# Forming the second gate inside the output projection instead of inside the second expert pass

## The chip, the core and the metric

The kernel runs on one core of one Trainium2 chip. The metric is the device time of one execution in microseconds; lower is better. The core's engines run side by side, each through its own instructions in order: PE (TensorE, the matmuls), DVE (VectorE), ACT (ScalarE), POOL (GpSimd) and SP (SyncE), which here only issues transfers. Sixteen DMA engines move data between main memory and the on-chip memory.

## What is computed

One layer of a decoder trunk on x of shape (1, 512, 2048). A conditioning vector c gives six rows of 2048 numbers (shift1, scale1, gate1, shift2, scale2, gate2), each a product of silu(c) with a 2048x2048 block of `w_ada`:

```python
mod = jax.nn.silu(c) @ w_ada[l] + b_ada[l]
shift1, scale1, gate1, shift2, scale2, gate2 = [m[:, None, :] for m in jnp.split(mod, N_MOD, axis=-1)]
h = x * (1.0 + scale1) + shift1
y = hybrid_mixer(h, ...)                        # ends with "@ w_out": the output projection
x = layer_norm(ALPHA * x + gate1 * y, ln1_g[l], ln1_b[l])
h = x * (1.0 + scale2) + shift2
y = peer(h, peer_w_q[l], peer_sub_keys[l], peer_u[l], peer_v[l])   # product-key experts
x = layer_norm(ALPHA * x + gate2 * y, ln2_g[l], ln2_b[l])
```

The second gate, gate2, is needed only for the last line.

## The kernel before

The program is one long stream, written in order and placed on the engines by a scheduler that keeps each engine's own sequence fixed. Its stages, with the times they take in the profile: input modulation, projection, state-space heads and attention (0 to about 586 us); the output projection (586 to about 800); the queries of the expert layer (to about 1000); the first expert pass with `uT` (to about 2137); the second expert pass with `vT` (to about 3187); the last LayerNorm.

All large matmuls use float32 data cut into two parts. `split` copies a raw tile to `hi` on ACT (L189) and forms `lo = raw - hi` on DVE (L190); `mm3` then runs three matmuls (L196 to L198). So each chunk of weights needs a transfer, one ACT pass, one DVE pass, and then PE work.

**`ada`** forms one row of the modulation on DVE. It walks a column piece of `w_ada` in sixteen slices of 128 rows: SP loads a slice (L220, tile `wa`), DVE multiplies it by one number per partition and adds it to the accumulator `acc` (L225 for the first slice, L227 for the others). For a gate, PE then sums `acc` over the partitions (L243, tile `pc`), DVE adds the bias (L244, tile `grow`) and the row goes to main memory. `ada` is a generator: each `pump` lets it do one step, so its work is laid between other work. `pace[0]` ties a step behind the latest `lo`.

**The output projection** (L738 to L784) runs over eight groups, one for each pair of token blocks and each of four column blocks `dc`. A group has eight steps; a step loads 512 KB of `w_out` (L745, tile `wo`, a ring of four buffers), splits it and runs 24 matmuls of 512 columns into `po`. At a group's end DVE runs `t`, `xres` and `stats` (L771 to L774). `norm1` (L699 and on) normalises finished token blocks between the steps. From the second group on each step adds `RATE_S` to a counter and pumps the generator `shifting` by its whole part. `shifting` is the second half of shift2: sixteen slices of 512 KB, through a ring of two buffers (`ra0`, `ra1`), the slots that the tag "rawa" names in this stage.

**The second expert pass** (L1133 on) runs sixteen rounds `sg`; a round has four column blocks `dc` of two parts. A part loads 1 MB of `vT` (L1144, tile `wvv`) into the three-buffer ring "raw8", splits it in two halves (L189, L190) and runs 36 matmuls into `pv`. Between them DVE adds finished blocks to `yacc` (L1195), and adds rows that POOL gathers one by one (L857) to `h2t` (L822). Before the change, in rounds 2 to 9, each first part also pumps `gate2`, an `ada` over column pieces of 512, whose loads hold four slices each (1 MB) and take a buffer of the same ring "raw8".

Of the kernel before, what the change touches and what calls it, by code (L numbers as in the profile page):

```python
# [21 lines left out]
D = 2048  # L22
# [9 lines left out]
SHARE = (4, 4, 8, 8)  # L32
RATE_X = 2
RATE_Z = 2.5
RATE_S = 0.6
EARLY_Q = 6
TAIL = ((0, 1, 2, 3), (0, 2), (0,))
G_SCALE = 32768.0
# [77 lines left out]
def body(ctx, tc, I, out, dbg=None):  # L116
# [7 lines left out]
    ps = Ring()  # L124
# [10 lines left out]
    st = Ring()  # L135
# [28 lines left out]
    g2s = tc.dram_tile([1, D], F32, name="g2s")  # L164
# [82 lines left out]
    def run(gen):  # L247
        for _ in gen:
            pass

    pace = [None]

    def pump(gen, n):
        for _ in range(n):
            if next(gen, gen) is gen:
                return


    with ExitStack() as sa:
        mx = sa.enter_context(tc.tile_pool(name="mx", bufs=1))  # L260
        rt = Tags(sa.enter_context(tc.tile_pool(name="rt", bufs=2)), bT=1, cT=1, xdt=1, btok=1, cbm=1, hst=1, sc=1, sq=2, ada=1)
# [70 lines left out]
        due = [0.0]  # L332
# [27 lines left out]
        pieces = WAVE  # L360
# [317 lines left out]
    with ExitStack() as sb:  # L678
# [10 lines left out]
        hf = xb.tile([P, D], F32, name="hf")  # L689
        shifting = ada(st, ps, rt, 3, 2, shift2, 0.0, ((1024, 1024),))  # L690

        def queries(hc):

            if hc % 2 == 0:
                early_q.append(ps.tile([P, 512], F32, name="pq", tag="acc"))
            at = hc % 2 * 2 * P
            colgemm2(I["w_q"][hc], early_q[-1][:, at:at + 2 * P], 0, 2 * P, False)
# [40 lines left out]
        for tbs, dc in [(t, d) for t in ((0, 1), (2, 3)) for d in range(4)]:  # L738
            dsl = slice(dc * 512, (dc + 1) * 512)
            t1 = {}  # L740
            for half in (1, 0):
                pa = {b: ps.tile([P, 512], F32, name=f"po{b}", tag="acc") for b in tbs}
                for q in range(4):
                    raw = st.tile([P, 2, 512], F32, name="wo", tag="raw")
                    nc.sync.dma_start(raw, I["w_out"][dc, half * 2 + q // 2][:, q % 2 * 2:q % 2 * 2 + 2, :])  # L745
                    hi, lo, ins = split(st, raw, [P, 2, 512], "w")
                    pace[0] = ins.ins
                    for b in tbs:
                        sl = slice(b * P, (b + 1) * P)
                        for k in range(2):  # L750
                            kk = (1 - half) * 8 + q * 2 + k
                            mm3(pa[b], hhi[:, kk, sl], hlo[:, kk, sl], hi[:, k, :], lo[:, k, :],
                                q == 0 and k == 0, q == 3 and k == 1)
                    if dc or tbs[0]:
                        due[0] += RATE_S
                        pump(shifting, int(due[0]))
                        due[0] -= int(due[0])
                if tbs[0] and dc == 3 and half == 0:
                    for hc in range(EARLY_Q):
                        queries(hc)  # L760
                if half == 1:
                    if tbs[0] == 0:
                        nc.scalar.dma_start(g1[:, dsl], g1s[0:1, dsl].to_broadcast([P, 512]))
                    for b in tbs:
                        nc.scalar.dma_start(xres[:, b, dsl], I["x"][b * P:(b + 1) * P, dsl])
                for b in tbs:
                    if half == 1:
                        t1[b] = rt.tile([P, 512], F32, name="t1", tag="t1")
                        A.activation(t1[b], pa[b], AF.Copy, scale=rms[:, 4 + b:5 + b])
                        continue  # L770
                    V.scalar_tensor_tensor(t1[b], pa[b], rms[:, b:b + 1], t1[b], ALU.mult, ALU.add)  # L771
                    V.tensor_tensor(t1[b], t1[b], g1[:, dsl], ALU.mult)
                    V.scalar_tensor_tensor(xres[:, b, dsl], xres[:, b, dsl], ALPHA, t1[b], ALU.mult, ALU.add)
                    V.bn_stats(stats[:, b, dc, :], xres[:, b, dsl])  # L774
                    if dc == 3 and b >= 2:
                        norm1(b)
            if tbs[0] and dc == 0:
                run(shifting)
                V.tensor_tensor(gc, cols[:, C_L1G:C_L1G + 16], scale2, ALU.mult)
                V.tensor_tensor(bc, cols[:, C_L1B:C_L1B + 16], scale2, ALU.mult)  # L780
                V.tensor_tensor(bc, bc, shift2, ALU.add)
                norm1(0)
            if tbs[0] and dc == 1:
                norm1(1)  # L784


    front.close()
# [73 lines left out]
    with ExitStack() as sc_:  # L861
# [30 lines left out]
        for hc in range(16):  # L892
            pa = ps.tile([P, 512], F32, name="pa", tag="acc")
            c0 = 2 * P if hc < EARLY_Q else 0
# [156 lines left out]
        for i in range(U1):  # L1051
            hl = dense_u(i)
# [8 lines left out]
    with ExitStack() as sv:  # L1061
# [67 lines left out]
        ws[1] = weights(1)  # L1129
        bring(3)  # L1130
        g2 = None
        gate2 = ada(st, ps, rt, 5, 1, g2s, pieces=tuple((c0, 512) for c0 in range(0, D, 512)), n=4, tag="raw8")
        for sg in range(16):  # L1133
            last = sg == 15
            for dc in range(4):
# [4 lines left out]
                for part in range(2):  # L1140
                    gi = sg * 2 + part
                    hl = []
                    both = st.tile([P, 4, 512], F32, name="wvv", tag="raw8")
                    nc.sync.dma_start(both, I["vT"][gi, dc])  # L1144
                    for n in range(2):
                        raw = both[:, 2 * n:2 * n + 2, :]
                        if final and part + n == 2:
                            hi = rt.tile([P, 2, 512], F32R, name="hi", tag="w")
                            lo = rt.tile([P, 2, 512], F32R, name="lo", tag="gt")
                            hl.append((hi, lo, split_into(hi, lo, raw)))  # L1150
                        else:
                            hl.append(split(st, raw, [P, 2, 512], "w"))
                    hls += hl
                    if final:
                        continue
                    for b in range(ND):
                        sl = slice(b * P, (b + 1) * P)
                        for i in range(4):
                            hi, lo = hl[i // 2][:2]
                            mm3(pa[b], ws[gi][:, 0, i, sl], ws[gi][:, 1, i, sl], hi[:, i % 2, :], lo[:, i % 2, :],  # L1160
                                part == 0 and i == 0, part == 1 and i == 3)
                    if sg < 15 and (dc, part) in ((1, 1), (3, 1)) and sg * 2 + 4 + dc // 2 < 32:
                        bring(sg * 2 + 4 + dc // 2)
                    if not last and (dc, part) in ((1, 0), (3, 0)):
                        nx = sg * 2 + 2 + dc // 2
                        ws[nx] = weights(nx)
                    if sg > 1 and part == 0:
                        pace[0] = hl[1][2].ins
                        pump(gate2, 1)
                    if sg < 14:  # L1170
                        for n in range(1 + (part + dc == 4 or (sg % 4, dc, part) == (0, 1, 0))):
                            fetch(hl[n][1].bitcast(F32)[:, 0, 0:1], hl[1][2].ins, 1)
# [105 lines left out]
```

## Time and profile before

| | |
|---|---|
| runs of the kernel | 3220.56 us median of 3 (3210.94 to 3221.17) |
| the profiled execution | 3211.76 us, of which span 3210.1 us |
| PE busy | 3072.1 us (96% of the span) |
| DVE busy | 2626.2 us (82%) |
| ACT busy | 1292.0 us (40%) |
| POOL busy | 801.4 us (25%) |
| loads of `wa` by SP | 96 of 512 KB, 48 of 1 MB |

The profile is of one execution: each row of its trace is an engine's instructions, transfers, or the time in which an engine stood still and what ended the wait. A busy PE is not a PE at its peak, since matmuls overlap and their ends are modelled; the number of matmuls in a stretch says more than the busy share. The profiled execution is near the fastest of the three runs, 8.80 us under their median.

### The profile page before, as it was taken

Reading aid. Unit: us, or ns where it says so; the run is one execution under the profiler, and the core shown is the slowest. Engines: PE = TensorE matmul, PEld = TensorE weight load, DVE = VectorE, ACT = ScalarE, POOL = GpSimd, SP = SyncE. Lnnn points to the kernel's source line nnn. Section 1 sums busy time; section 2 is a strip of 40 time slices with the busy share of each in tenths; the row PEclk is TensorE's granted clock in tenths of the full one; section 3 lists DMA queues with packets and bytes.
Section 4 is the critical chain, followed back from the end, with each engine's and each line's share of the span. In section 5 each row is a group of like instructions: output and inputs, shape, how many; then the busy total and the mean of one; then the engine's idle time right before and its main releaser. Section 6 shows DMA issues by size and latency. Waiting matters only on the chain.

```text
span 3210.1 us, 43195 instructions
## 1 busy us (share of the span) xinstructions
PE 3072.1 (96%) x16241; PEld 2622.1 (82%) x16241; DVE 2626.2 (82%) x4091; ACT 1292.0 (40%) x2149; POOL 801.4 (25%) x651
## 2 busy tenths in 40 slices
PE   7889899899799999999999998999999999999997
PEld 3677577678788999999999998988777778788885
DVE  6677877686597999999999896868888889888887
ACT  2333335445422333475467774333222232223332
POOL 0000001001240154333432232322434334533301
PEclk9989999999899999999999999999999999999998
DMA  9654654586653599989998889998999989898862
GB/s 341 222 172 149 212 178 137 173 285 196 215 189 112 212 345 351 339 317 364 334 345 327 329 330 350 395 339 314 333 342 330 340 325 365 327 350 314 308 230 79
DMA packets 249426, 899.92 MB, mean 280 GB/s; under 512 B 19600, under 2 KB 113744, under 8 KB 173280
## 3 DMA queue, kind: packets, MB, share of 16 engines
q1 hardware_dynamic: 106624, 460.46, 39.7%
q0 software_dynamic: 41776, 303.12, 25.1%
q10 hardware_dynamic: 100816, 133.57, 12.4%
q8 instruction: 127, 2.08, 0.3%
q14 instruction: 83, 0.68, 0.1%
HBM read 834.87 MB, written 62.19 MB: 279 GB/s over the span
## 4 chain that ended last, share of the span: by engine, by line
PE 75%; DVE 8%; DMA 8%; issue 5%; POOL 1%; ACT 1%; SPq 0%; DVEq 0%; ACTq 0%; POOLq 0%
PE pa L198 11%; PE pa L196 11%; PE pa L197 11%; PE pv L197 9%; PE pv L198 9%; PE pv L196 9%; DMA wa<-w_ada 3%; DMA wvv<-vT 3%; DVE lo L190 2%; PE po L197 1%; PE po L198 1%; PE pg L1011 1%; PE po L196 1%; DVE acc L227 1%; POOL row L857 1%
## 5 line engine op out<-in xcount | busy, mean ns | idle before, releaser
L196 PE MATMUL pa<-hhi,hi 128*128 128x352 f32 (+2 forms) x2656 | 906.0, 341 | 18.4 <-ACT hi L189 18.4
L198 PE MATMUL pa<-hhi,lo 128*128 128x352 f32 (+2 forms) x2656 | 903.9, 341 | 9.4 <-DVE lo L190 9.4
L197 PE MATMUL pa<-hlo,hi 128*128 128x352 f32 (+2 forms) x2656 | 902.3, 340 | 0.0
L854 POOL COPY row<-lo 128x1 f32<-128x1 f32 x288 | 240.9, 836 | 1265.5 <-DVE lo L190 623.3
L196 PEld LDWEIGHTS pa<-hhi,hi 128*128 128x128 f32 x2656 | 504.1, 190 | 43.0 <-ACT hi L189 19.6
L198 PEld LDWEIGHTS pa<-hhi,lo 128*128 128x128 f32 x2656 | 503.1, 190 | 35.6 <-DVE lo L190 12.2
L189 ACT CAST hi<-wvv 128x1024 fp32r<-128x1024 f32 x256 | 265.2, 1051 | 647.3 <-PE pv L198 507.9
L197 PEld LDWEIGHTS pa<-hlo,hi 128*128 128x128 f32 x2656 | 504.3, 190 | 22.9 <-issue 3.5
L189 ACT CAST hi<-wu 128x1024 fp32r<-128x1024 f32 x300 | 311.5, 1046 | 508.0 <-PE pa L197 411.8
L190 DVE TENSOR_TENSOR lo<-wu,hi 128x1024 fp32r<-128x1024 f32 x300 | 379.0, 1272 | 128.9 <-ACT hi L189 120.7
L190 DVE TENSOR_TENSOR lo<-wvv,hi 128x1024 fp32r<-128x1024 f32 x256 | 309.3, 1223 | 122.3 <-ACT hi L189 79.6
L197 PE MATMUL pv<-lo,wpr 128*128 128x512 f32 x1008 | 393.1, 391 | 2.9 <-DVE lo L190 2.9
L198 PE MATMUL pv<-hi,wpr 128*128 128x512 f32 x1008 | 392.2, 390 | 0.0
L196 PE MATMUL pv<-hi,wpr 128*128 128x512 f32 x1008 | 376.7, 391 | 4.8 <-ACT hi L189 4.8
L822 DVE SCALAR_TENSOR_TENSOR h2t<-row,adot,h2t 128x2048 f32<-128x2048 f32 x127 | 297.6, 2343 | 3.4 <-DMA row<-v,exi 2.8
L818 DVE SCALAR_TENSOR_TENSOR row<-row,h2t 128x2048 f32<-128x2048 f32 x128 | 292.0, 2284 | 4.8 <-DMA row<-u,exi 4.8
L857 POOL DMA_INDIRECT row<-v,exi x128 | 223.1, 1743 | 37.7 <-POOL row L854 35.7
L196 PEld LDWEIGHTS pv<-hi,wpr 128*128 128x128 f32 x1008 | 189.0, 188 | 49.2 <-ACT hi L189 7.3
L197 PEld LDWEIGHTS pv<-lo,wpr 128*128 128x128 f32 x1008 | 189.6, 188 | 45.6 <-DVE lo L190 5.9
L198 PEld LDWEIGHTS pv<-hi,wpr 128*128 128x128 f32 x1008 | 189.7, 188 | 39.7
L197 PE MATMUL pv<-lo,wp 128*128 128x512 f32 x528 | 209.6, 398 | 2.1 <-DVE lo L190 2.1
L198 PE MATMUL pv<-hi,wp 128*128 128x512 f32 x528 | 209.0, 397 | 0.0
(328 smaller groups left out, 4663.3 us busy)
## 6 DMA issues: line engine op xcount, KB each, us to landing
wu<-uT SPq DMA_DIRECT2D x128, 1024.0 KB
wvv<-vT SPq DMA_DIRECT2D x128, 1024.0 KB
wa<-w_ada SPq DMA_DIRECT2D x48, 1024.0 KB
wa<-w_ada SPq DMA_DIRECT2D x96, 512.0 KB
wo<-w_out SPq DMA_DIRECT2D x64, 512.0 KB
gds<-gq ACTq DMA_DIRECT2D x12, 2048.0 KB
gt<-gds ACTq DMA_DIRECT2D x32, 768.0 KB
wi<-w_in SPq DMA_DIRECT2D x44, 512.0 KB
```

The costliest lines, as they stand in the source:

```text
L189: A.copy(hi, raw)
L190: return V.tensor_tensor(lo, raw, hi.bitcast(F32), ALU.subtract)
L196: T.matmul(ps, lh, rh, start=start, stop=False)
L197: T.matmul(ps, lh, rl, start=False, stop=False)
L198: return T.matmul(ps, ll, rh, start=False, stop=stop)
L227: V.scalar_tensor_tensor(acc, raw[:, kt - k0, :], cs[:, kt:kt + 1], acc, ALU.mult, ALU.add)
L818: V.scalar_tensor_tensor(row, row, 1.0, h2t, ALU.mult, ALU.mult, accum_out=adot[:, e:e + 1])
L822: V.scalar_tensor_tensor(gacc, row, adot[:, e:e + 1], gacc, ALU.mult, ALU.add)
L854: G.tensor_copy(row[:, 0:1], pace)
L857: G.indirect_dma_start(out=row, out_offset=None, in_=I["u" if n < X + P else "v"], in_offset=bass.IndirectOffsetOnAxis(ap=at, axis=0))
L1011: T.matmul(pg[:, (k % 2 * 2 + tt) * P:(k % 2 * 2 + tt + 1) * P], oj[:, tt, :], oi[:, tt, n, :], start=n == 0, stop=n == 1)
```

## The change

`gate2` is taken out of the second expert pass. In the output projection a generator `rows2` runs `shifting` and behind it an `ada` for the gate with its default form: two column pieces of 1024, 32 loads of 512 KB through the two-buffer ring "rawa". `RATE_S` goes from 0.6 to 0.9. What is left of `rows2` at the stage's end is run there.

```diff
-RATE_S = 0.6
+RATE_S = 0.9
...
         shifting = ada(st, ps, rt, 3, 2, shift2, 0.0, ((1024, 1024),))
+
+        def rows2():
+            yield from shifting
+            yield from ada(st, ps, rt, 5, 1, g2s)
+
+        turns = rows2()
...
                     if dc or tbs[0]:
                         due[0] += RATE_S
-                        pump(shifting, int(due[0]))
+                        pump(turns, int(due[0]))
                         due[0] -= int(due[0])
...
             if tbs[0] and dc == 1:
                 norm1(1)
+        run(turns)
...
         g2 = None
-        gate2 = ada(st, ps, rt, 5, 1, g2s, pieces=tuple((c0, 512) for c0 in range(0, D, 512)), n=4, tag="raw8")
...
-                    if sg > 1 and part == 0:
-                        pace[0] = hl[1][2].ins
-                        pump(gate2, 1)
```

On SP, the queue that issues the loads, the program before ends the projection with 28 loads of `wo` in a row, and lays a load of `wa` between every three to five loads of `wvv` in the second pass:

```order
L220 DMA wa<-w_ada 128x1024
L745 DMA wo<-w_out 128x1024 x28
L669 DMA wu<-w_q 128x1024 x12
L663 DMA wu<-w_q 128x2048 x16
L663 DMA wu<-uT 128x2048 x128
L1144 DMA wvv<-vT 128x2048 x17
L220 DMA wa<-w_ada 128x4x512
L1144 DMA wvv<-vT 128x2048 x3
L220 DMA wa<-w_ada 128x4x512
L1144 DMA wvv<-vT 128x2048 x3
```

In the changed program the same queue has, from the end of the projection on:

```order
L751 DMA wo<-w_out 128x1024
L220 DMA wa<-w_ada 128x1024
L751 DMA wo<-w_out 128x1024
L220 DMA wa<-w_ada 128x1024
L669 DMA wu<-w_q 128x1024
L220 DMA wa<-w_ada 128x1024 x2
L669 DMA wu<-w_q 128x1024 x11
L663 DMA wu<-w_q 128x2048 x16
L663 DMA wu<-uT 128x2048 x128
L1150 DMA wvv<-vT 128x2048 x121
```

The loads of `wa` stand between the loads of `wo` to the projection's end, and none is left among the loads of `wvv`.

On DVE, in the seventh group of the projection (the third column block of the second pair of token blocks), the program before has the steps' `lo` back to back up to the evictions `t` of the group's first half:

```order
L773 SCALAR_TENSOR_TENSOR xres<-xres,t_5528 128x512
L717 TENSOR_SCALAR hT<-pt,gc,bc 128x128
L774 BN_STATS stats<-xres 128x6
L190 TENSOR_TENSOR lo<-wo,hi 128x1024
L774 BN_STATS stats<-xres 128x6
L190 TENSOR_TENSOR lo<-wo,hi 128x1024 x6
L771 SCALAR_TENSOR_TENSOR t_5752<-po_5756,rms,t_5752 128x512
```

The changed program has there:

```order
L190 TENSOR_TENSOR lo<-wo,hi 128x1024
L227 SCALAR_TENSOR_TENSOR acc<-wa,cs,acc 128x1024
L190 TENSOR_TENSOR lo<-wo,hi 128x1024
L227 SCALAR_TENSOR_TENSOR acc<-wa,cs,acc 128x1024
L723 TENSOR_SCALAR hT<-pt,gc,bc 128x128
L190 TENSOR_TENSOR lo<-wo,hi 128x1024
L227 SCALAR_TENSOR_TENSOR acc<-wa,cs,acc 128x1024
L190 TENSOR_TENSOR lo<-wo,hi 128x1024
L227 SCALAR_TENSOR_TENSOR acc<-wa,cs,acc 128x1024
L190 TENSOR_TENSOR lo<-wo,hi 128x1024
L777 SCALAR_TENSOR_TENSOR t_5835<-po_5839,rms,t_5835 128x512
```

Between two `lo` there now stands one accumulation. Counted over the eight steps of each group, the accumulations were 0, 4, 5, 5, 2, 0, 0, 0 and are now 0, 4, 8, 8, 8, 4, 8, 8.

## Rows read from the trace of the kernel before

**Rows 1.** The page: busy time, share and instructions of each engine; and the shares of the chain of work that ended last.

```profile
PE 3072.1 (96%) x16241; PEld 2622.1 (82%) x16241; DVE 2626.2 (82%) x4091; ACT 1292.0 (40%) x2149; POOL 801.4 (25%) x651
...
PE 75%; DVE 8%; DMA 8%; issue 5%; POOL 1%; ACT 1%; SPq 0%; DVEq 0%; ACTq 0%; POOLq 0%
```

**Rows 2.** Busy time in two stretches of the second expert pass, each cut where a round's first `lo` begins: rounds 2 to 9, and rounds 10 to 13. Columns: stretch, its length, busy time and instructions of PE, PEld, DVE, ACT, POOL; then the granted clock, the DMA share and GB/s.

```profile
2229.85:2785.85 556.00, 542.73 (x2327) 434.03 (x2326) 477.92 (x400) 159.39 (x162) 226.68 (x150) 1.00 0.91 335
2785.85:3048.90 263.05, 263.05 (x1149) 215.53 (x1148) 220.71 (x168) 80.09 (x80) 93.68 (x76) 1.00 0.88 326
```

**Rows 3.** The same stretches, instructions that read or write `wvv` alone (DVE: `lo`, sixteen to a round; ACT: `hi`).

```profile
2229.85:2785.85 556.00, 154.19 (x128) 132.37 (x129) 1.00 0.91 335
2785.85:3048.90 263.05, 77.89 (x64) 66.74 (x64) 1.00 0.88 326
```

**Rows 4.** The same stretches, instructions of `pv` alone (first PE, the matmuls; then PEld, DVE, ACT).

```profile
2229.85:2785.85 556.00, 539.07 (x2319) 433.69 (x2318) 63.06 (x96) 0.00 (x0) 1.00 0.91 335
2785.85:3048.90 263.05, 263.05 (x1149) 215.53 (x1148) 31.74 (x48) 0.00 (x0) 1.00 0.88 326
```

**Rows 5.** The same stretches, DVE's additions of gathered rows (L822) alone.

```profile
2229.85:2785.85 556.00, 177.89 (x76) 1.00 0.91 335
2785.85:3048.90 263.05, 91.39 (x40) 1.00 0.88 326
```

**Rows 6.** Who waited for whom in rounds 2 to 9: us in total, times, longest.

```profile
ACT hi L189 <- PE pv L198: 223.1, 45, 15.1
...
ACT hi L189 <- DMA wvv<-vT: 107.3, 32, 8.9
```

**Rows 7.** The longest wait of ACT in rounds 10 to 13, where no wait on `wvv` is listed.

```profile
ACT hi L189 <- PE pv L198: 168.2, 55, 5.9
```

**Rows 8.** Groups of instructions in rounds 2 to 9: the gate's sums on PE and its bias on DVE (busy us, mean ns; idle before).

```profile
L243 PE MATMUL pc<-acc,ones 128*1 128x512 f32 x8 | 4.1, 591 | 0.5 <-DVE acc L227 0.5
L244 DVE TENSOR_TENSOR grow<-pc,grow 1x512 f32<-1x512 f32 x4 | 2.7, 672 | 0.0
```

**Rows 9.** SP's issues in the second pass, in order of time (start, length of the run of issues).

```profile
2351.58 36.13 SPq L1144 DMA_DIRECT2D wvv<-vT  x5
2391.32 0.38 SPq L220 DMA_DIRECT2D wa<-w_ada  x1
2397.18 18.11 SPq L1144 DMA_DIRECT2D wvv<-vT  x3
```

**Rows 10.** The output projection by groups, cut where a group's first `lo` begins: groups 2 to 8 of eight (columns as in rows 2).

```profile
629.00:653.50 24.50, 22.82 (x90) 17.76 (x91) 18.81 (x21) 9.46 (x11) 0.00 (x0) 0.93 0.96 340
653.50:677.00 23.50, 22.61 (x97) 17.80 (x97) 20.32 (x22) 9.69 (x10) 0.00 (x0) 1.00 0.87 285
677.00:699.70 22.70, 22.40 (x97) 17.74 (x96) 20.20 (x21) 9.70 (x10) 0.00 (x0) 1.00 0.87 294
699.70:726.50 26.80, 25.16 (x124) 20.30 (x123) 22.23 (x43) 11.65 (x17) 1.30 (x1) 1.00 0.78 264
726.50:752.20 25.70, 25.70 (x130) 21.33 (x129) 17.09 (x22) 18.89 (x34) 7.45 (x4) 1.00 0.61 202
752.20:776.70 24.50, 23.47 (x103) 18.56 (x103) 16.79 (x19) 13.40 (x19) 5.64 (x3) 1.00 0.55 177
776.70:799.70 23.00, 23.00 (x102) 18.74 (x102) 15.51 (x17) 9.69 (x10) 0.00 (x0) 1.00 0.60 194
```

**Rows 11.** Groups of DVE instructions from 629 to 800 us.

```profile
L190 DVE TENSOR_TENSOR lo<-wo,hi 128x1024 fp32r<-128x1024 f32 x56 | 70.1, 1254 | 41.8 <-ACT hi L189 41.5
L227 DVE SCALAR_TENSOR_TENSOR acc<-wa,cs,acc 128x1024 f32<-128x1024 f32 x15 | 19.2, 1278 | 0.0
...
L717 DVE TENSOR_SCALAR hT<-pt,gc,bc 128x128 f32<-128x128 f32 x8 | 3.2, 404 | 0.9 <-ACT hT L714 0.8
```

**Rows 12.** The chain of work that ended last, in order of time, where it runs through loads of `wa` into the same two-buffer ring, before the projection (start, us, what; for a load from its issue to its landing).

```profile
194.75 5.38 DMA wa<-w_ada
200.16 1.28 DVE acc L227
201.47 4.64 DMA wa<-w_ada
206.13 1.29 DVE acc L227
207.45 5.18 DMA wa<-w_ada
...
360.13 3.72 DMA wa<-w_ada
...
462.88 6.17 DMA wa<-w_ada
...
480.22 3.79 DMA wa<-w_ada
```

**Rows 13.** Busy time in stretches that hold those loads (columns as in rows 2).

```profile
195.00:225.00 30.00, 26.67 (x133) 21.84 (x131) 22.90 (x44) 7.38 (x11) 0.00 (x0) 0.98 0.81 261
455.00:480.00 25.00, 24.47 (x156) 19.36 (x154) 18.11 (x27) 10.14 (x22) 2.54 (x2) 1.00 0.47 148
```

**Rows 14.** What ACT waited for most from 629 to 800 us.

```profile
ACT hi L189 <- PE po L198: 66.8, 44, 3.0
```

## The prediction

> **What bounds the kernel now.** I read the page first: PE is busy 96% of the span and carries 75% of the chain that ended last [rows 1]. So PE sets the end almost everywhere, and the change can only matter through PE's waits in the two places that it touches. Both must be priced apart: time that the second expert pass gives back, and time that the output projection takes.
>
> For the pass I cut the trace at the rounds' first `lo`, so that rounds 2 to 9, with the gate, stand beside rounds 10 to 13, which run the same code without it. The counts of `lo` (128 and 64) show eight and four rounds [rows 3]. A round takes 556.00 / 8 = 69.5 us with the gate and 263.05 / 4 = 65.8 us without. DVE's gathered rows are no lighter in the later rounds, 40 in four against 76 in eight [rows 5]. With the gate PE stands idle 556.00 - 542.73 = 13.3 us; without, never [rows 2]. The waits say why: with the gate ACT waits 107.3 us in 32 places for the landing of `wvv`; without it only for PE [rows 6, 7]. The queue shows the mechanism: `wa` takes one of the three buffers of 1 MB in the `wvv` loads' own ring, and SP, which issues in order, stands in front of it [rows 9].
>
> For the projection I cut at the groups. PE is busy nearly throughout, and ACT's cast waits mostly for PE to free a `hi` [rows 10, 14]. DVE is the next engine: it is busy 20.20 of 22.70 us in the fourth group, with five accumulations, but only 15.51 of 23.00 in the eighth, with none [rows 10].
>
> **What the pass gives back.** The change removes 16 loads of 1 MB, 64 accumulations and the sums on PE. Three prices bound it. By work done: 2319 matmuls of `pv` in 556.00 us against 1149 in 263.05 [rows 4]; at the later rate the 2319 would take 530.9 us, so 25.1 us come back. By the rounds' length: 8 x (69.5 - 65.8) = 29.9 us. By PE's visible standstill alone: 13.3 us and the 4.1 us of the gate's sums [rows 2, 8], 17.4 us. I take 25, since a count of matmuls doesn't hang on where DVE stood at the cut. DVE's relief itself is worth nothing here, as it has idle time in these rounds (477.92 of 556.00 busy) [rows 2]. What is late next is PE, as rows 7 show. So -25 us, between -29.9 and -17.4.
>
> **What the projection pays.** The order of DVE gives, for groups 2 to 8, 4, 8, 8, 8, 4, 8, 8 accumulations where there were 4, 5, 5, 2, 0, 0, 0: 32 more, at 1.278 us each [rows 11], 40.9 us of DVE. The gate's four biases (0.672 us each [rows 8]) come with them. Added to DVE's busy time of each group [rows 10]:
>
> - group 3: 20.32 + 3 x 1.28 = 24.2 of 23.50 us
> - group 4: 20.20 + 3.8 = 24.0 of 22.70
> - group 5: 22.23 + 7.7 = 29.9 of 26.80 (0.4 less, since one `hT` moves to a later group [rows 11])
> - group 6: 17.09 + 5.1 + 0.7 for a bias, less 0.4 = 22.5 of 25.70, room left
> - group 7: 16.79 + 10.2 + 0.7 + 0.8 for two `hT` = 28.5 of 24.50
> - group 8: 15.51 + 10.2 = 25.7 of 23.00
>
> So DVE becomes the bound in five of the seven groups. Packed without a gap it costs 0.7 + 1.3 + 2.7 + 4.0 + 2.7 = 11.4 us. That is the low end.
>
> There is a second limit: the ring of two buffers. A load for step n can be issued only when the accumulation two before it is done, so two accumulations take at least a landing and one accumulation. Earlier in the same trace the same ring binds just so: the chain runs load, accumulation, load, accumulation, with landings of 5.38, 4.64 and 5.18 us, down to 3.72 and up to 6.17; the 17 from 194.75 to 480.22 us have a mean of 4.82 [rows 12]. Those stretches moved 261 and 148 GB/s [rows 13]; the projection already moved 285 to 294 with five accumulations a group [rows 10], and one `wo` and one `wa` of 512 KB in 3.5 us would be 300. Loads share the DMA engines, so I take a landing near the upper end, 5.7 us. Then an accumulation takes (5.7 + 1.28) / 2 = 3.49 us, and eight of them 27.9 us. Behind each late `wa` on DVE's queue stands the next `lo`, and PE waits for that.
>
> The Trainium skill, page "DMA: Bandwidth & Descriptors", section "Anatomy of one DMA", has a fit of 2.0 us and the bytes over 436 GB/s. For 512 KB that gives an estimate of 3.2 us, and the ring would need (3.2 + 1.28) / 2 = 2.24 us an accumulation and never bind; by it the projection would pay the 11.4 us, and the sum be the first rival's. The landings of this trace are all longer, and the measurement decides.
>
> A group takes the longer of the two. Where DVE is longer (groups 5 and 7) I add 2.5 us, DVE's idle time in the best packed group (22.70 - 20.20). That gives 27.9, 27.9, 32.0, 25.7, 31.0 and 27.9 us for groups 3 to 8 against 23.50, 22.70, 26.80, 25.70, 24.50 and 23.00: 4.4 + 5.2 + 5.2 + 0 + 6.5 + 4.9 = 26.2 us. The second group, with the same four accumulations, is left alone. The gate's sums, 4.1 us of PE [rows 8], are hidden while PE waits for DVE; without that cover they come on top. High end: a landing of 6.17 gives 3.73 us and 29.8 a group of eight, 6.3 + 7.1 + 5.2 + 0 + 6.5 + 6.8 = 31.9, and 4.1 makes 36.0. So +26 us, between +11.4 and +36.
>
> Two small edits cost nothing by themselves: SP's own issues (0.38 us each [rows 9]) fit between its waits, and shift2 is ready a group earlier, which `norm1` in group 5 can't use, since it waits for that group's statistics.
>
> **The sum.** -25 + 26 = +1 us on 3211.76, 3212.8. The profiled execution lies 8.8 us under the median of the runs, 3220.56, on which the same sum gives 3221.6. I give the middle, 3217 us. The runs of this kernel spread over 10 us, so 0.3% (9.7 us) is about what a measurement can tell from no change. My forecast is no change that can be told.
>
> **The rivals.** Each from 3216, the middle of the two bases.
>
> - *The ring doesn't bind* (faster). Landings stay under 4.8 us, DVE is packed without gaps, and the projection pays 11.4: -25 + 11.4 = -13.6, 3202 us. For it: in the projection so far no accumulation waited for its load (idle before, 0.0 [rows 11]). Against it: there the accumulations were five a group, and the ring had 4.6 us for each.
> - *Landings get long* (slower). The projection's second group already moved 340 GB/s at a DMA share of 0.96 [rows 10]. If the two interleaved streams hold the engines there, a landing grows and DVE's whole queue with it. Five groups of eight cost 40p - 120.5 us at p us an accumulation (120.5 is the five groups' length before); it decides when this passes 25 + 9.7, so from p = 3.88, a landing of 6.5 us. At 7 us p is 4.14 and the cost 45: +20, 3236 us. Against it: a slower step also asks for less traffic, and no landing of rows 12 is over 6.17.
> - *The pass gives less* (no change or slightly slower). Only the 17.4 us of visible standstill return, because the 1 MB loads still meet the gathered rows on the DMA engines, whose share is 0.88 even without the gate [rows 2]: +9, 3225 us. Against it: the later rounds have that same traffic and PE never stands still.
>
> **How the numbers follow.** Chances: forecast 0.40 (same 0.37, faster 0.01, slower 0.02), first rival 0.25 (faster 0.22, same 0.03), second 0.27 (slower 0.25, same 0.02), third 0.08 (half same, half slower). Together faster 0.23, same 0.46, slower 0.31. The range reaches from the best ends on the profile's base, 3211.76 - 29.9 + 11.4 = 3193, to the worst on the median's, 3220.56 - 17.4 + 36 = 3239; I cut it to 3195 to 3238. The forecast alone has 3207 to 3227.
>
> **What the next profile would show.** Right: rounds 2 to 9 at about 66 us with no wait of ACT on `wvv`; 32 more accumulations before 850 us; groups 3 to 8 about 26 us longer together, with DVE busy nine tenths and idle time before the accumulations that ends with `wa`. Wrong on the ring: accumulations of the projection without a wait on `wa`, and groups of 24 to 26 us. Wrong on the pass: waits on `wvv` that stay, or rounds over 68 us. The prediction as a whole fails if one side moves by more than 10 us against the other.

## The result, and the profile after

The change makes the kernel slower: 3233.52 us (median of 17 runs, 3219.17 to 3250.25) against 3216.62 us (17 runs, 3206.21 to 3225.47), a ratio of 1.0054 with a 95% interval of 1.0042 to 1.0066. That is 16.9 us, where the sum had given 1 us and "no change" the largest chance. It lies inside the stated range, but above the 3207 to 3227 us of the forecast alone. The profiled execution after has a span of 3224.2 us, that of before 3210.1: 14.1 us more.

**The pass.** Rounds 2 to 9 and rounds 10 to 13 of the second expert pass in the kernel after, cut as before at a round's first `lo` (stretch, length, busy time and instructions of PE, PEld, DVE, ACT, POOL; granted clock, DMA share, GB/s):

```profile
2266.40:2797.10 530.70, 529.32 (x2305) 432.46 (x2304) 439.28 (x334) 161.30 (x160) 167.43 (x152) 1.00 0.87 322
2797.10:3063.10 266.00, 266.00 (x1162) 218.01 (x1161) 218.52 (x167) 82.62 (x82) 80.46 (x75) 1.00 0.87 318
```

The longest wait of ACT in rounds 2 to 9; none on `wvv` is listed any more:

```profile
ACT hi L189 <- PE pv L198: 330.3, 106, 7.4
```

Beside [rows 2, 6]: rounds 2 to 9 are 25.3 us shorter (530.70 against 556.00), PE stands idle 1.4 us instead of 13.3, and the wait on `wvv` of 107.3 us is gone. Rounds 10 to 13, which run the same code in both, came out 2.95 us longer (over all the profiles here they took from 263.0 to 272.4 us, so that is spread). The pass as a whole is shown by one row, the first and the last start of its 256 `lo` (times of start at the end of the row), here of the kernel after:

```profile
L190 DVE TENSOR_TENSOR lo<-wvv,hi x256: 1206/1224/1262, 2129.2 to 3184.7; 128x1024 fp32r<-128x1024 f32 x128
```

and the same row of the kernel before:

```profile
L190 DVE TENSOR_TENSOR lo<-wvv,hi x256: 1207/1220/1267, 2091.2 to 3170.5; 128x1024 fp32r<-128x1024 f32 x128
```

It starts 38.0 us later and ends 14.2 later, so 23.8 us come back (1055.5 against 1079.3 us).

**The projection.** Groups 2 to 8, cut at a group's first `lo`, and behind them groups 3 to 8 in one stretch (columns as above):

```profile
629.00:652.50 23.50, 22.83 (x90) 17.71 (x91) 18.71 (x21) 9.66 (x10) 0.00 (x0) 0.93 0.99 353
652.50:679.30 26.80, 23.62 (x99) 17.79 (x98) 23.88 (x24) 9.67 (x10) 0.00 (x0) 1.00 0.87 302
679.30:709.30 30.00, 26.37 (x121) 20.73 (x119) 23.67 (x27) 10.41 (x11) 0.00 (x0) 1.00 0.91 308
709.30:740.50 31.20, 23.68 (x92) 17.51 (x92) 28.52 (x47) 10.14 (x15) 0.00 (x0) 0.95 0.84 268
740.50:768.20 27.70, 26.44 (x124) 20.51 (x124) 22.49 (x26) 17.04 (x28) 7.06 (x4) 1.00 0.88 318
768.20:798.70 30.50, 28.46 (x126) 21.13 (x125) 27.95 (x30) 16.23 (x26) 7.08 (x4) 1.00 0.85 286
798.70:829.00 30.30, 23.81 (x89) 16.78 (x88) 24.16 (x26) 9.65 (x10) 0.00 (x0) 0.94 0.79 267
652.50:828.95 176.45, 152.33 (x644) 114.44 (x643) 150.62 (x174) 73.14 (x98) 14.14 (x8) 0.98 0.85 291
```

The last of these in the kernel before:

```profile
653.50:798.61 145.11, 141.25 (x641) 113.56 (x641) 111.04 (x141) 73.03 (x98) 14.38 (x8) 1.00 0.71 236
```

It ends at 798.61 us, where the queries' first `lo` begins, and not at the 799.70 of [rows 10], which is 1.1 us too late by the rule given there: group 8 took 21.9 us before, not 23.0. (A step of the projection runs 12 matmuls into `po`, two token blocks by two chunks by three, and not 24; so the counts of PE are near 96 where a group has no other work.) Behind the groups come the queries, of which the first twelve `lo` stand in the same loop, and the first expert pass. Their `lo` before (shortest, middle and longest in ns, first and last start):

```profile
L190 DVE TENSOR_TENSOR lo<-wu,hi x12: 1164/1224/1873, 798.6 to 832.2; 128x1024 fp32r<-128x1024 f32 x12
L190 DVE TENSOR_TENSOR lo<-wu,hi x256: 1172/1220/1259, 1012.2 to 2087.5; 128x1024 fp32r<-128x1024 f32 x128
```

and after:

```profile
L190 DVE TENSOR_TENSOR lo<-wu,hi x12: 1212/1225/1476, 829.0 to 866.2; 128x1024 fp32r<-128x1024 f32 x12
L190 DVE TENSOR_TENSOR lo<-wu,hi x256: 1179/1218/1273, 1044.9 to 2125.4; 128x1024 fp32r<-128x1024 f32 x128
```

So groups 3 to 8 take 176.5 us where they took 145.1: +31.4. Group 2 is 1.0 us shorter. The first twelve chunks of the queries take 37.2 us for 33.6, +3.6; the rest of the queries is 1.3 us shorter. The first expert pass, up to the second's first `lo`, is 5.3 us longer, and the second 23.8 shorter. The account is -1.0 + 31.4 + 3.6 - 1.3 + 5.3 - 23.8 = 14.2 us, the 14.1 of the span but for rounding. The 5.3 us of the first pass are not the change's: a kernel of before without the gate (e4 below) took 1084.8 us for it, as after did (1084.3), and the 1079.0 of before is the shortest of all the profiles here.

**What PE waits for there.** The longest waits of PE, PEld and DVE that concern the question, from 629 to 829 us after (us in total, times, longest):

```profile
PEld po L197 <- DVE lo L190: 32.2, 28, 4.0
PE po L197 <- DVE lo L190: 21.6, 22, 3.6
DVE acc L227 <- DMA wa<-w_ada: 16.5, 16, 2.6
```

and the two that there were from 629 to 800 us before, where no accumulation waited for its load:

```profile
PEld po L197 <- DVE lo L190: 9.3, 14, 1.4
PE po L197 <- DVE lo L190: 4.0, 7, 1.0
```

PE and its weight loads waited 13.3 us for `lo`, added up over both, and now 53.8. (They wait side by side, so the sum is a measure and not a time; PE itself stands idle 24.7 us in groups 2 to 8 after, 199.9 less the 175.2 that it is busy, and 5.5 before.) How a late load gets there is seen in DVE's timeline after, at the end of group 4 (start, length, and in brackets the idle time before and what ended it):

```profile
704.65 1.22 DVE L190 TENSOR_TENSOR lo<-wo,hi 128x1024 fp32r<-128x1024 f32 x1
708.10 1.28 DVE L227 SCALAR_TENSOR_TENSOR acc<-wa,cs,acc 128x1024 f32<-128x1024 f32 x1 [2.23 <-DMA wa<-w_ada]
709.30 1.22 DVE L190 TENSOR_TENSOR lo<-wo,hi 128x1024 fp32r<-128x1024 f32 x1
```

and in PE's at the same place:

```profile
710.58 0.51 PE L197 MATMUL po<-lo,hhi 128*128 128x512 f32 x1 [1.61 <-DVE lo L190]
```

DVE stands 2.23 us for a `wa`, then accumulates for 1.28, and only then forms the `lo`, which PE awaits. And at a column piece's end DVE waits for PE's sum, for which the forecast had no price: 2.06 us ahead of `shift`, as the same timeline has it some us earlier, and 1.2 us once for the gate:

```profile
697.98 0.17 DVE L235 SCALAR_TENSOR_TENSOR shift<-pc,cols 128x8 f32<-128x8 f32 x1 [2.06 <-PE pc L233]
```

### The profile page after: what moved, and what is told of

Same layout as the page of the kernel before. It is cut to its first block, busy times and chain, and to the rows that moved or that the text cites. A ratio compares the mean times of both kernels' runs of the same rounds, so it can differ in the third digit from the quotient of the medians.

```text
span 3224.2 us, 43242 instructions
## 1 busy us (share of the span) xinstructions
PE 3078.8 (95%) x16241; PEld 2628.7 (82%) x16241; DVE 2627.8 (82%) x4059; ACT 1296.1 (40%) x2149; POOL 733.5 (23%) x651
## 3 DMA queue, kind: packets, MB, share of 16 engines
q0 software_dynamic: 41776, 303.12, 25.1%
## 4 chain that ended last, share of the span: by engine, by line
PE 73%; DMA 8%; DVE 8%; issue 7%; POOL 2%; ACT 1%; ACTq 0%; DVEq 0%; SPq 0%; POOLq 0%
PE pa L198 11%; PE pa L196 11%; PE pa L197 11%; PE pv L197 10%; PE pv L198 10%; PE pv L196 10%; DMA wa<-w_ada 5%; DVE lo L190 2%; DVE acc L227 2%; POOL row L864 2%; DMA w<-gas 1%; PE pg L1018 1%; PE pw L196 1%; DMA gds<-gq 1%; PE pw L197 1%
## 5 line engine op out<-in xcount | busy, mean ns | idle before, releaser
L198 PE MATMUL pa<-hhi,lo 128*128 128x352 f32 (+2 forms) x2656 | 906.9, 342 | 13.3 <-DVE lo L190 13.3
L197 PEld LDWEIGHTS pa<-hlo,hi 128*128 128x128 f32 x2656 | 505.8, 190 | 22.8 <-issue 3.5
L861 POOL COPY row<-lo 128x1 f32<-128x1 f32 x288 | 172.0, 597 | 1317.8 <-DVE lo L190 724.1
L198 PE MATMUL pv<-hi,wpr 128*128 128x512 f32 x1008 | 391.7, 390 | 0.0
L196 PE MATMUL pv<-hi,wpr 128*128 128x512 f32 x1008 | 386.8, 390 | 0.0
```

The source lines that it names most:

```text
L196: T.matmul(ps, lh, rh, start=start, stop=False)
L197: T.matmul(ps, lh, rl, start=False, stop=False)
L198: return T.matmul(ps, ll, rh, start=False, stop=stop)
L861: G.tensor_copy(row[:, 0:1], pace)
```

## The experiments

Each was timed beside the kernel before. "Groups" are groups 2 to 8 of the projection together in its profile, to the queries' first `lo`: 169.6 us before (170.7 in the expectations, with the late end of [rows 10]), 199.9 after. "Pass" is the time from the pass's first to its last `lo`: 1079.3 and 1055.5 us. e1, e2, e3, e9 and e10 are edits of the kernel after, the others of the kernel before.

**e4: the gate left out altogether.** The bound for both sides: before, without the gate's loads, accumulations and sums.

```diff
-        gate2 = ada(st, ps, rt, 5, 1, g2s, pieces=tuple((c0, 512) for c0 in range(0, D, 512)), n=4, tag="raw8")
...
-                    if sg > 1 and part == 0:
-                        pace[0] = hl[1][2].ins
-                        pump(gate2, 1)
...
-                g2 = big(g2s[0:1, :].to_broadcast([P, D]))
+                g2 = big(I["bg"][1:2, :].to_broadcast([P, D]))
```

> The kernel before without the second gate's loads, accumulations and sums; its row is the bias alone, so that part of the computation is left out. It shows what the gate costs in the second expert pass. Theory: rounds 2 to 9 take 530 us instead of 556, no wait of ACT on wvv, the projection is unchanged, and the whole is 22 to 26 us faster than the kernel before, about 3193 us. Rival (the pass has another limit, the gathered rows): under 12 us faster.

Measured: 0.9940 [0.9923, 0.9958], 19.3 us, a little under what was expected. Rounds 2 to 9 of e4, in the view of busy times:

```profile
2233.50:2761.20 527.70, 527.70 (x2305) 432.59 (x2304) 439.60 (x333) 161.74 (x160) 160.78 (x152) 1.00 0.88 324
```

The pass takes 1053.3 us. The gate's whole cost in the pass is thus 26.0 us by the profiles and 0.60%, 19.3 us, by the runs. The change, at 1055.5, gets nearly all of it back. It also gives a floor for the projection: after stands 1.0054 - 0.9940 = 1.14%, 37 us, over e4, and that is what the gate costs there, everything counted, the higher `RATE_S` too. (A difference of two such ratios is sure to about 0.2%, 7 us.)

**e7 and e8: is it the loads or the accumulations in the pass?** e7 reads one held tile in place of the gate's 16 loads and keeps the 64 accumulations; e8 keeps the loads and cuts 60 of the 64 accumulations to 8 columns.

```diff
 e7
-        gate2 = ada(st, ps, rt, 5, 1, g2s, pieces=tuple((c0, 512) for c0 in range(0, D, 512)), n=4, tag="raw8")
+        held_w = wv.tile([P, 1, 512], F32, name="heldw")
+        nc.sync.dma_start(held_w, ...)
+        gate2 = ada(st, ps, rt, 5, 1, g2s, pieces=tuple((c0, 512) for c0 in range(0, D, 512)), n=4, tag="raw8", held=held_w)
 e8
-                            V.scalar_tensor_tensor(acc, raw[:, kt - k0, :], cs[:, kt:kt + 1], acc, ALU.mult, ALU.add)
+                            V.scalar_tensor_tensor(acc[:, :cut], raw[:, kt - k0, :cut], cs[:, kt:kt + 1], acc[:, :cut],
+                                                   ALU.mult, ALU.add)
...
-        gate2 = ada(st, ps, rt, 5, 1, g2s, pieces=tuple((c0, 512) for c0 in range(0, D, 512)), n=4, tag="raw8")
+        gate2 = ada(st, ps, rt, 5, 1, g2s, pieces=tuple((c0, 512) for c0 in range(0, D, 512)), n=4, tag="raw8", cut=8)
```

> The kernel before, where the second gate's loads in the pass are left out: its 64 accumulations read one tile loaded once, so the gate's values are not the gate. Theory A (the wvv ring): rounds 2 to 9 fall to about 532 us and the whole is 15 to 20 us faster than before. Theory B1 (DVE's work costs it): they stay at 550 us or more.

> The kernel before with all of the gate's 1 MB loads in the wvv ring, but 60 of its 64 accumulations take 8 columns of 512; the other columns of the gate are left out. Theory A (the wvv ring): rounds 2 to 9 stay at 548 us or more, with the wait of ACT on wvv near 100 us. Theory B1 (DVE's work): they fall to about 532 us.

Measured: e7 0.9956 [0.9941, 0.9972], e8 0.9981 [0.9970, 0.9992]. Rounds 2 to 9 of e7:

```profile
2231.45:2764.61 533.16, 531.54 (x2311) 432.46 (x2311) 478.79 (x400) 161.54 (x160) 199.83 (x152) 1.00 0.86 321
```

and of e8, with the wait on `wvv` that it keeps in the second fence:

```profile
2229.68:2780.26 550.58, 540.53 (x2325) 436.53 (x2325) 447.52 (x400) 160.00 (x162) 237.47 (x150) 0.99 0.91 338
```

```profile
ACT hi L189 <- DMA wvv<-vT: 106.8, 32, 8.0
```

Without the loads 22.8 of the 28.3 us between before and e4 go, though DVE is as busy as before (478.79 us). With the loads and a DVE that is 30 us less busy, 5.4 go, and the wait of 107 us stays as it was. So the pass pays mainly for the loads. By the runs they are 0.44% of the 0.60% (e7), and DVE's work is 0.16% to 0.19% (e7 against e4, and e8), 5 to 6 us.

**e5: the loads stay, but leave the `wvv` ring.** The gate stays in the pass with all its work, through three buffers of its own of 256 KB, one k tile to a load.

```diff
-        gate2 = ada(st, ps, rt, 5, 1, g2s, pieces=tuple((c0, 512) for c0 in range(0, D, 512)), n=4, tag="raw8")
+        class Small:
+            turn = 0
+            def tile(self, shape, dt, name, tag):
+                self.turn += 1
+                if self.turn % 3 == 0:
+                    return wv.tile(shape, dt, name=name, tag="g0", bufs=1)
+                return rt.tile(shape, dt, name=name, tag="lrow")
+        gate2 = ada(Small(), ps, rt, 5, 1, g2s, pieces=tuple((c0, 512) for c0 in range(0, D, 512)), n=1)
...
-                    if sg > 1 and part == 0:
+                    if sg > 1:
```

> The kernel before, with the second gate still in the second expert pass, but its loads no longer take buffers of the wvv ring: 64 loads of 256 KB go through three small buffers of their own, one accumulation a part from round 2 on. All of the work is done. Theory A (the wvv ring's lost buffer costs the 25 us): the wait of ACT on wvv, 107 us before, falls under 15, rounds 2 to 9 take about 532 us instead of 556, and the whole is 15 to 20 us faster than the kernel before, so faster than both kernels. Theory B (DVE's work or the 16 MB of traffic costs it): rounds 2 to 9 stay at 550 us or more and the time within 6 us of the kernel before.

Measured: 0.9956 [0.9941, 0.9971], 14 us faster than before, and 1.0% faster than the change. The longest wait of ACT in rounds 2 to 9 of e5; none on `wvv` is listed:

```profile
ACT hi L189 <- PE pv L198: 295.3, 99, 12.4
```

The rounds take 539.4 us, not the 532 of the expectation, and the pass 1064.2 us. The same bytes cross the same DMA engines as before, and most of the loss goes, so it was not paid for the bytes. By the runs e5 is level with e7, which makes no loads at all. But e5 changes more than the ring: its loads are a quarter as large and stand evenly, one in each part. What the freed buffer gives and what the smaller loads give is not taken apart by any run; that the lost buffer is the main thing is argued from ACT's wait on `wvv`, which goes.

**e1, e2, e3: which limit makes the projection long?** Each takes one limit from the kernel after. e1 gives the ring four buffers; e2 leaves the gate's 32 loads out (one held tile); e3 cuts 30 of the gate's 32 accumulations to 8 columns and keeps the loads.

```diff
 e1
-        st.slots["rawa"] = [(xb, "ra0"), (xb, "ra1")]
+        st.slots["rawa"] = [(xb, f"ra{n}") for n in range(4)]
 e2
-            yield from ada(st, ps, rt, 5, 1, g2s)
+            yield from ada(st, ps, rt, 5, 1, g2s, held=held_w)
 e3
-            yield from ada(st, ps, rt, 5, 1, g2s)
+            yield from ada(st, ps, rt, 5, 1, g2s, cut=8)
```

> The changed kernel with four buffers instead of two in the ring of wa in the output projection. Theory A (the two-buffer ring): DVE's standstill before accumulations, 16.5 us in 16 places in the changed kernel, falls under 3 us, the seven groups take about 184 us instead of 200, and the whole is about 15 us faster than the changed kernel, level with the kernel before. Theory B (DVE's added work alone): the standstill before wa goes but DVE waits for ACT or PE instead, groups stay near 197 us, and the time stays within 5 us of the changed kernel. Theory C (the traffic of 16 MB more): as B, and landings grow beyond 6 us since more loads are in flight.

> The changed kernel, where the 32 loads of the second gate are left out: all 32 accumulations read one tile that is loaded once, so the gate's values are not the gate. Theory B (DVE's added work): the seven groups still take 185 us or more, 15 us or more over the 170.7 of the kernel before. Theories A and C (ring or traffic): they fall to 175 us or less, and the time is 25 us under the changed kernel's, about 8 us faster than the kernel before.

> The changed kernel with all its loads, but 30 of the second gate's 32 accumulations take 8 columns instead of 1024; the other columns of the gate are left out. Theory B (DVE's added work): the seven groups fall to 175 us or less, about 25 us under the changed kernel. Theory C (traffic): they stay at 190 us or more, with PE or DVE waiting for wo or wa. Theory A (ring): with a landing of 5.2 us and a short accumulation the ring needs 2.7 us a load, under the 3.4 us of a step, so it agrees here with B.

Measured: e1 1.0006 [0.9994, 1.0019], e2 1.0029 [1.0015, 1.0042], e3 0.9971 [0.9957, 0.9985]. The groups of DVE's accumulations in the projection, e1 (count, busy us, mean ns; idle before, and what ended it):

```profile
L227 DVE SCALAR_TENSOR_TENSOR acc<-wa,cs,acc 128x1024 f32<-128x1024 f32 x45 | 58.9, 1308 | 0.1
```

of e2:

```profile
L230 DVE SCALAR_TENSOR_TENSOR acc<-wa,cs,acc 128x1024 f32<-128x1024 f32 x15 | 19.2, 1279 | 3.3 <-DMA wa<-w_ada 3.1
```

and of e3 (both lengths in one row):

```profile
L227 DVE SCALAR_TENSOR_TENSOR acc<-wa,cs,acc 128x8 f32<-128x8 f32 (+1 forms) x45 | 27.2, 606 | 25.5 <-DMA wa<-w_ada 25.2
```

With four buffers the wait on `wa` is gone, 16.5 us to 0.1, and 0.48%, 15 us, of the 37 with it. e1 thus met the time that theory A expected, but not the length of the groups, 191.6 us against the 184 expected: 30.7 of them lie in group 2, which took 23.5 after. e3 has the time that theory B expected, 27 us under after, and against B its groups are still 192.2 us long, with a wait on `wa` of 25.2 us. e2 gave 8 us and groups of 195.4, as B had it for the groups; the waits that it still has (3.1 us) are those of `shift2`'s own loads through two buffers at the higher rate. Neither theory, one limit alone, fits all three.

**e9 and e10: both limits taken.** e9 is e1 and e3 together, e10 is e1 and e2 together.

> The changed kernel with four buffers in the wa ring and, for 30 of the gate's 32 accumulations, 8 columns instead of 1024; the rest of the gate is left out, all loads are made. Both suspected limits of the projection are gone, only the 16 MB of traffic is left. Theory (ring and DVE's work are all of it): the seven groups take 175 us or less and the time is 15 to 20 us under the kernel before, as without the gate. Rival (traffic): groups 182 us or more, time within 10 us under the kernel before.

> The changed kernel with four buffers in the wa ring and without the gate's 32 loads: all its accumulations read one tile that is loaded once, so the gate's values are not the gate. Only DVE's added work is left. Theory: groups about 190 us, as with four buffers and all loads, and the time within 4 us of that kernel's, which was level with the kernel before. Rival (traffic weighs beside the ring): 8 us or more faster than that kernel.

Measured: e9 0.9960 [0.9944, 0.9976], e10 1.0005 [0.9990, 1.0020]. Groups 2 to 8 of e9 in one stretch, and its group 2 by itself:

```profile
629.10:808.60 179.50, 170.28 (x738) 131.57 (x739) 139.79 (x196) 82.39 (x108) 12.38 (x8) 0.99 0.92 333
...
629.10:657.20 28.10, 23.81 (x90) 17.65 (x91) 22.47 (x23) 9.44 (x10) 0.00 (x0) 0.94 1.01 369
```

e10 is level with e1, so with four buffers the loads themselves cost nothing that the runs can tell, and all that e1 still pays is DVE's work. e9, where neither limit is left, is within 0.2% of the kernel without any gate. The 179.5 us of its groups and its 13 us under before lie between what the theory (175 us or less, 15 to 20 us) and what the rival, traffic, expected. They are 9.9 us over before. Nearly 4 of them lie in group 2, with four buffers and a DMA share of 1.01. Another 4.1 can be the gate's sums, which e9 still runs on PE:

```profile
L244 PE MATMUL pc<-acc,ones 128*1 128x512 f32 x8 | 4.1, 591 | 0.0
```

So little is left for the traffic. Groups 3 to 8 of e1, e3 and e9, each in one stretch:

```profile
655.70:816.60 160.90, 149.32 (x647) 114.68 (x646) 146.50 (x172) 73.31 (x98) 15.20 (x8) 0.99 0.87 305
652.70:821.04 168.34, 152.52 (x650) 115.44 (x649) 119.96 (x177) 73.04 (x98) 12.46 (x8) 0.98 0.89 304
657.20:808.62 151.42, 146.49 (x650) 113.94 (x649) 117.32 (x174) 72.94 (x99) 12.38 (x8) 1.00 0.90 327
```

Side by side (the waits of PE and PEld for `lo` added from each profile's list of waits over groups 2 to 8, PE's waits by other names left out; cost over e4 from the ratios):

| | ring of two | DVE's work | groups 2 to 8, us | groups 3 to 8, us | PE and PEld wait for `lo`, us | over e4 |
|---|---|---|---|---|---|---|
| after | yes | yes | 199.9 | 176.5 | 53.8 | 1.14%, 37 us |
| e1 | no | yes | 191.6 | 160.9 | 27.2 | 0.66%, 21 us |
| e3 | yes | no | 192.2 | 168.3 | 34.1 | 0.31%, 10 us |
| e9 | no | no | 179.5 | 151.4 | 15.0 | 0.20%, 6 us |

If a group took the longer of the two limits, after would be about as long as the longer of e1 and e3. (Not quite, because the forecast's ring term holds an accumulation; by its own numbers that makes 2.3 us over e1, as worked out below.) It is 15.6 us longer than e1 and 8.2 us longer than e3 in groups 3 to 8, and 15 and 27 us in the runs. Over e9, groups 3 to 8 pay 9.5 us for DVE's work alone, 16.9 for the ring alone and 25.1 for both: they come near to adding. In the runs the three are 15, 4 and 30 us, more than the sum, though four ratios leave an error of some 9 us on that. Why they add is seen in groups 4 and 8 (further below): DVE's queue is in order, so its waits for loads and its own work follow each other.

The short accumulations also tell what made the queries start slower. The first twelve `lo` of the queries in e10, with DVE's work, and in e3, without it:

```profile
L190 DVE TENSOR_TENSOR lo<-wu,hi x12: 1216/1225/1476, 820.4 to 857.7; 128x1024 fp32r<-128x1024 f32 x12
L190 DVE TENSOR_TENSOR lo<-wu,hi x12: 1164/1224/1874, 821.0 to 854.6; 128x1024 fp32r<-128x1024 f32 x12
```

They take 36.1 to 37.3 us in after, e1, e2 and e10, and 33.6 in all the other kernels here, e3 and e9 among them. So the 3.6 us come with DVE's added work.

**e6 and e11: the rate by itself.** `RATE_S` 0.9 in the kernel before (e6), and in e5 (e11).

```diff
-RATE_S = 0.6
+RATE_S = 0.9
```

> The kernel before with RATE_S 0.9 alone: shift2 is pressed into fewer steps of the output projection, the gate stays in the pass. Theory: groups 3 and 4 grow by 4 to 7 us each as in the changed kernel, what follows has the work already behind it and gets 4 us back, so the whole is 4 to 8 us slower. Rival (shift2's early end frees norm1): as fast as before or faster.

> The second gate in the pass through its own three small buffers (as in the earlier run, 0.44% faster than the kernel before) and RATE_S 0.9 for shift2 (alone 0.16% faster, interval 0.02 to 0.29). All of the work is done. If both add: 0.5 to 0.7% faster than the kernel before, about 3196 us. If the rate's gain was chance: 0.4 to 0.5%.

Measured: e6 0.9984 [0.9971, 0.9998], e11 0.9947 [0.9927, 0.9966]. e6 was expected 4 to 8 us slower, and that was a miss. Its groups 3 and 4, with eight accumulations each, did grow to 27.3 and 26.8 us, and group 5 shrank to 24.4: 173.8 us together against 169.6. Yet the runs are a little faster, and why isn't settled. e11 can't be told from e5. e5 and e11 beat before and after, with all work done.

## Why the prediction was wrong

**The pass: the mechanism right, the size 6 us too large by the runs.** The term was -25. In the profile rounds 2 to 9 gave 25.3 and the whole pass 23.8, but by the runs of e4 it is 19 us, near the small end of the stated range, 17.4. The mechanism was the one read from SP's order and ACT's wait: e7 and e8 show that the gate's loads make up about three quarters of its cost, and in e5 the wait on `wvv` goes once they leave its ring. DVE's relief was put at nothing; e8 finds 5.4 us in the profile and 0.19% in the runs for it.

**The landings: right.** 5.7 us were taken from [rows 12]. Three of the loads of `wa` in the chain of work that ended last, after (start, us from issue to landing):

```profile
663.91 4.81 DMA wa<-w_ada
...
723.05 5.88 DMA wa<-w_ada
...
739.76 6.76 DMA wa<-w_ada
```

The ten that the chain has from 652.5 to 829 us have a mean of 5.75, from 4.81 up to 6.76. The first rival, that the ring doesn't bind, is gone with that. The forecast's estimate of 3.2 us goes back to the Trainium skill, page "DMA: Bandwidth & Descriptors", section "Anatomy of one DMA — SWDGE (gpsimd) path". As that heading says, the fit is for transfers that GpSimd issues. The loads here are issued by SP, so the fit did not apply to them, and the 5.75 us neither bear it out nor refute it.

**The step that failed: "A group takes the longer of the two".** In groups 3, 4 and 8 DVE's work gave 24.2, 24.0 and 25.7 us and the ring 27.9, which was taken; in groups 5 and 7 DVE's work was taken alone, with 2.5 us of idle time. Groups 3 to 8 were forecast at 27.9, 27.9, 32.0, 25.7, 31.0, 27.9 and measured 26.8, 30.0, 31.2, 27.7, 30.5, 30.3. The forecast is too low just in group 4 (2.1), group 8 (2.4) and group 6 (2.0). In 4 and 8 the ring was longer by the rule, but there DVE's work and its waits stand one behind the other. Its waits in group 4 (the first two lines) and in group 8:

```profile
DVE acc L227 <- DMA wa<-w_ada: 4.6, 5, 2.2
DVE shift L235 <- PE pc L233: 2.1, 1, 2.1
...
DVE acc L227 <- DMA wa<-w_ada: 4.6, 4, 2.6
```

In group 4 DVE is busy 23.67 us, which with 4.6 and 2.1 of waiting makes the group's 30.0 to within 0.4; in group 8 it is 24.16 and 4.6 of 30.3. In group 6 nothing was to be paid, since four accumulations had "room left", 3.2 us of it. It paid 2.0: PE stood idle 1.3 us, nearly all of it for `lo`, and ran two of the gate's sums, 1.0 us, which the forecast had as hidden. By the rule a deeper ring would have been worth 2.3 us (DVE's work and 2.5 us in every group give 23.9 in place of 26.2). e1 measured 15.6 us in groups 3 to 8, of which 7.2 go back in group 2, and 15 us in the runs.

**What was not in the sum.** The first twelve chunks of the queries are 3.6 us longer, and the forecast ended at the last group; e3 and e10 show that this too is DVE's work. The late end of [rows 10] hid 1.1 us of group 8's growth. So the profile lies 13 us over the sum, 14.1 for 1, by 5.2 us of groups 3 to 8 (31.4 for 26.2: 4.1 by the rule, 1.1 by the late end), 3.6 of the queries' start, 5.3 of spread in the first pass and 1.2 less from the second (-23.8 for -25), less 2.3 of small differences. In the runs the projection's side is 37 us against 26 in the sum, just over the high end of 36, and the pass's 19 against 25. Both errors point the same way, and 1 us became 17. The larger part, 11 us, is the projection's.

**The rivals.** The result fell on the side of the second, but not by its mechanism. That one needed an accumulation to take more than 3.88 us in the five groups of eight, by landings of 6.5 us. They took 26.8 + 30.0 + 31.2 + 30.5 + 30.3 = 148.8 us, 3.72 each. The third, that the pass returns only PE's 17.4 us of standstill, is refuted in the profile by 25.3 us, while the runs' 19 us do not exclude it.

**What stays open.** Why e6 isn't slower; how much of the 0.20% that e9 pays over e4 is traffic (the two intervals, and the 4.1 us of sums, leave room for none); and that groups 3 to 8 of e3 are 7.4 us longer in its profile than those of e1, though its runs are 0.35% shorter. A single profile may lie some microseconds off its kernel's median (that of e3 lies 9.5 over, that of e1 5 under), so between e1 and e3 the runs decide and the windows don't.

## What to carry to other kernels

A stream of loads that is put into another stream's ring costs that stream a buffer. That was dear here, and the bytes were not: three small buffers of its own, filled by smaller loads (e5), got back 14 of the 19 us without moving any work. In this case DVE's own work and a short ring behind it did not hide one another. So before taking the longer of two such limits, price their sum too, group by group, or give the ring the depth that lets it run ahead (two more buffers took 15 us off here), and follow a late engine into the stage behind the one that is changed.

## What the runs showed of the hardware

Some of DVE's operations took longer beside work of POOL on tiles. POOL's `hlo` after, from 784.03 us, and what DVE did meanwhile (timeline of all engines, start and length):

```profile
784.03 3.85 POOL L727 TENSOR_TENSOR hlo<-hT,hhi 128x512 fp32r<-128x512 f32 x2 [3.86 <-ACT hhi L726]
...
784.75 1.99 DVE L190 TENSOR_TENSOR lo<-wo,hi 128x1024 fp32r<-128x1024 f32 x1
...
786.66 2.31 DVE L227 SCALAR_TENSOR_TENSOR acc<-wa,cs,acc 128x1024 f32<-128x1024 f32 x1
```

The `lo` took 1.99 us where others beside it took 1.22, and the accumulation 2.31 where 1.28 is usual. Of the 120 accumulations of 1024 columns in this trace, the nine beside a `TENSOR_TENSOR` of POOL took 1.27 to 2.31 us, and none of the others more than 1.29; so such a meeting can cost, and need not. In groups 6 and 7, where POOL is busy 7 us each and which had no accumulations before, their mean is 1.54 us, and over all groups it rose from 1.278 us [rows 11] to 1.342:

```profile
L227 DVE SCALAR_TENSOR_TENSOR acc<-wa,cs,acc 128x1024 f32<-128x1024 f32 x11 | 16.9, 1539 | 3.4 <-DMA wa<-w_ada 3.4
```

That POOL's work is the cause was not tried by itself. An accumulation of 8 columns takes 221 ns where 512 columns take 745, as the row of e8 in the pass has it:

```profile
L227 DVE SCALAR_TENSOR_TENSOR acc<-wa,cs,acc 128x8 f32<-128x8 f32 x60 | 13.3, 221 | 0.3
```

And PE's granted clock, 1.00 in groups 3 to 8 of before, fell to 0.95 and 0.94 in groups 5 and 8 after, the two in which PE was busy for the smallest part (23.68 of 31.20 and 23.81 of 30.30 us). So for a part of these two groups the lower of its two levels, 1.2 GHz, was granted instead of 2.4. That PE's wait for DVE brought this about is read from these rows and was not tried.
